# First GLU group split into two blocks, transposes placed inside later products, and nine products on zeros ahead of the first

## The chip, the cores and the metric

The kernel runs on one core of one Trainium2 chip. The metric is the device time of one execution in microseconds, and the median of three runs is taken. TensorE (PE) has a clock gate with two levels, 1.2 and 2.4 GHz; the profile lists the granted share of the full clock.

## What is computed

One hybrid decoder layer on 256 tokens of width 2048, in float32:

```python
h = rmsnorm(x, pre_mix_norm[l])
z = h @ w_in[l]
conv_in, q_lat, kv_lat, k_rope = z[..., :c1], z[..., c1:c2], z[..., c2:c3], z[..., c3:]
a, g = jnp.split(conv_in, 2, axis=-1)
u = a * jax.nn.sigmoid(g)
u = causal_depthwise_conv(u, conv_w[l], conv_b[l])
u = jax.nn.silu(layernorm(u, conv_ln_g[l], conv_ln_b[l]))
q = (rmsnorm(q_lat, q_norm[l]) @ w_uq[l]).reshape(B, S, N_HEADS, QK_HEAD)
...
kv = (rmsnorm(kv_lat, kv_norm[l]) @ w_ukv[l]).reshape(B, S, N_HEADS, QK_NOPE + V_HEAD)
...
attn = causal_attention(q_full, k_full, v)
mix = jnp.concatenate([rmsnorm(u, conv_out_norm[l]),
                       rmsnorm(attn, attn_out_norm[l])], axis=-1) @ w_out[l]
x = x + rmsnorm(mix, post_mix_norm[l])
hf = rmsnorm(x, pre_ffn_norm[l])
ff = (jax.nn.silu(hf @ w_gate[l]) * (hf @ w_up[l])) @ w_down[l]
x = x + rmsnorm(ff, post_ffn_norm[l])
```

The conv has 1024 channels and 31 taps; there are 8 heads with 128 plain and 64 rotary query columns; the q latent has 768 columns, the kv latent 512.

## The kernel before

**Products.** Every operand is split into two float16 parts, high and low, whose sum is the operand. A weight arrives by DMA in pieces of at most 2048 columns by 128 partitions, in one of four stage buffers; ACT writes the high part (line 97) and DVE the low part (line 98) into eight pairs of buffers. `mm3` (lines 136 to 144) makes a token-major product: for each of 16 row tiles and each of two token blocks three matmuls (high by high, high by low, low by high), 96 matmuls for a product of 2048 rows. `mm3t` (lines 146 to 153) does the same feature-major. All weight DMAs are issued by SP, in one queue; a piece's DMA waits for a stage buffer, which is free when DVE has made the low part of four pieces before.

**Order of the early work.** In program order:
1. x transposed is loaded in pieces and split (lines 102 and 103, `load_x`) between the pieces of the first weight group, `wg0` (pieces of 1, 1, 2, 2, 2, 4 and 4 row tiles). Then `wg1` is loaded, and ahead of its third piece both halves of x by tokens (line 206), which the token norm needs (lines 248 to 254).
2. Four GLU groups of 512 columns (256 values and 256 gates, two channel blocks of 128). After a group's product, for each token block: tanh of the gates (line 298), a copy of the values (line 300), u = (tanh + 1) * values on DVE (line 302), two transposes on PE (line 305) into PSUM, and a copy into the padded channel-major buffer `upad` (line 306).
3. The conv works channel-major on `upad`. `conv_todo` is a list of tap tasks; a task is one tap on two channel blocks. Tap 0 runs on ACT (line 270); taps 4, 8, ... 28 are multiplied on ACT (line 281) and added on DVE (line 283, 512 columns at once); the others are one multiply-add on DVE for each block (line 275). `pump(n)` takes the next n tasks off the list, and `PUMPS` gives the counts by place: after the four GLU groups, after the three latent products, after the rotary queries, the values and each head.
4. Three latent products of 448 columns. Their columns are copied by ACT (line 348). The q latent's norm follows the second product, the kv latent's the third: sum of squares on ACT (line 328), rsqrt on GpSimd (line 196), scaling on DVE (line 330), a split, and a DMA transpose of each token block issued by SP (line 332).
5. The shared rotary key: seven small operations on DVE for each token block (lines 364 to 370), a transpose on PE (line 371), a copy (line 372). Then the rotary queries: one product of 36 matmuls, six DVE operations for each token block (lines 387 to 392), four transposes (line 395). Then the values: two products of 24 matmuls on the normed kv latent (lines 402 to 408).
6. Eight heads (projections, scores, softmax scaled by GpSimd on line 467, output), then output projection, layer norm of the conv output, and the feed-forward part. The feed-forward products take the time from about 310 us on.

**What sets the order.** The program text gives each instruction its priority; a planner orders each engine's queue when the program is built, by priority among what it holds to be ready at that time by its own costs. So PE's queue may hold transposes between products that come later in the text, and DVE's may hold later splits ahead of earlier taps. On the chip each queue runs in that fixed order, and an instruction that waits holds everything behind it.

Of the kernel before, what the change touches and what calls it, by code (L numbers as in the profile page):

```python
# [35 lines left out]
PUMPS = dict(conv=(3, 8, 13, 14), lat=(11, 16, 9), v=(1, 0), uqp=3, head=(2, 7, 4, 8, 4, 4, 9, 8))  # L36
# [5 lines left out]
# Exact power-of-two scales that centre the half-precision parts of an operand.  # L42
# [8 lines left out]
def hymba_layer(ctx: ExitStack, tc: tile.TileContext, x, xT, pos, inv_freq, g_pre, w_in, w_lat,  # L51
# [16 lines left out]
    def region(kb, shape, dtype=F32):  # L68
        """A part of the arena from kb KB on; parts with disjoint lifetimes share it."""
# [12 lines left out]
    def nm(base):  # L82
        uid[0] += 1
        return f"{base}_{uid[0]}"
# [15 lines left out]
    def split_g(hi, lo, src, g):  # L100
        """Split of src times a scalar per partition."""
        nc.scalar.activation(hi, src, AF.Copy, scale=g)  # L102
        nc.vector.scalar_tensor_tensor(lo, src, g, hi, op0=ALU.mult, op1=ALU.subtract)

    class Weights:
        """Columns of a weight, on chip as half-precision parts, in blocks of kpb row tiles."""
# [6 lines left out]
        def load(self, src, scale, first=None, before=None):  # L113
            """src: [P, kt * n] with row tile by row tile along the free axis."""
# [31 lines left out]
    def mm3t(ps, x_of, wgt, c0):  # L146
        """Feature-major product of 128 columns: ps += w[:, c0:c0+128].T @ x."""
# [43 lines left out]
    def rstd_of(ss, n, w=1, out_tile=None):  # L191
        """(ss / n + eps) ** -0.5"""
# [24 lines left out]
    ps0 = [acc_tile(), acc_tile()]  # L217
    mm3(ps0, h_of, wg0)
    pos_f = const.tile([P, NTB], F32, name="pos_f")
# [45 lines left out]
    def conv_tap(quarter, k):  # L265
        """One tap of a quarter of the channels, on the vector engine or shared with the scalar engine."""
        cbs = range(2 * quarter, 2 * quarter + 2)
# [15 lines left out]
        nc.vector.tensor_tensor(a, a, t, op=ALU.add)  # L283
# [5 lines left out]
    for j in range(4):  # L289
        if j == 0:  # L290
            ps = ps0
        else:
            wgt = wg1 if j == 1 else Weights(KD, 512).load(w_in[j], W_S)
            ps = [acc_tile(), acc_tile()]
            mm3(ps, h_of, wgt)
        for tb in range(NTB):
            th = work.tile([P, 256], F32, tag="A", name=nm("th"), bufs=3)
            nc.scalar.activation(th, ps[tb][:, 256:512], AF.Tanh, scale=r_half[:, tb : tb + 1])
            av = work.tile([P, 256], F32, tag="B", name=nm("av"), bufs=3)
# [476 lines left out]
```

## Time and profile before

| | us |
|---|---|
| runs: median, lowest, highest | 1021.41, 1021.18, 1021.69 |
| the profiled execution: span from first to last instruction | 1019.8 |
| PE busy (matmuls, pipelined) | 988.7 |
| DVE busy | 635.8 |
| ACT busy | 502.6 |
| GpSimd (POOL) busy | 37.2 |

The profiled execution has no time of its own on record beside its span; the span is 1.6 us under the median of the runs. In the rows, L142 is a line of the kernel, PEld is PE's weight load, which overlaps the matmuls, and a row of several instructions ends in x and their number. The duration of a matmul holds its way through the array, so matmuls that follow each other overlap on record. The idle time of an engine before an instruction, and what ended it, stand in square brackets.

### The profile page before, as it was taken

The numbers are of one execution on the slowest core, as the hardware profiler recorded it, in microseconds if no ns is written. First come the engines' busy times: TensorE is split into PE (matmuls) and PEld (weight loads), VectorE is DVE, ScalarE is ACT, GpSimd is POOL, SyncE is SP. The second block draws the span as 40 slices with busy tenths as digits, with TensorE's granted clock in tenths as the row PEclk, the third lists the DMA queues.
The fourth block names the chain that finished last, engine by engine and source line by source line (L and its number), as shares of the span: only waits on it lengthen the run. The fifth ranks groups of instructions, "written<-read, shape, count | busy, mean of one in ns | idle before, by whom it ended". The sixth has DMA issues, their size and how long they took to land.

```text
span 1019.8 us, 11876 instructions
## 1 busy us (share of the span) xinstructions
PE 988.7 (97%) x4712; PEld 468.2 (46%) x4712; DVE 635.8 (62%) x724; ACT 502.6 (49%) x577; POOL 37.2 (4%) x50
## 2 busy tenths in 40 slices
PE   6999997999999999999999999999999999999996
PEld 2444553774444444444444444444444444444442
DVE  6699999999859874555555555554455444454412
ACT  7796665664747564444444444444444333343400
POOL 0000000034100100000000000000000000000000
PEclk9999998999999999999999999999999999999998
DMA  9874666577546978667666766677766665556302
GB/s 345 326 258 141 220 210 193 165 248 239 174 165 170 294 287 298 210 206 223 216 215 218 220 218 217 218 203 228 214 209 208 213 204 204 202 207 206 124 1 83
DMA packets 69512, 214.21 MB, mean 210 GB/s; under 512 B 41808, under 2 KB 42448, under 8 KB 47440
## 3 DMA queue, kind: packets, MB, share of 16 engines
q1 hardware_dynamic: 68736, 212.52, 63.6%
q8 instruction: 37, 0.61, 0.3%
q10 hardware_dynamic: 720, 0.93, 0.3%
q14 instruction: 19, 0.16, 0.0%
HBM read 202.16 MB, written 2.10 MB: 200 GB/s over the span
## 4 chain that ended last, share of the span: by engine, by line
PE 74%; DVE 11%; issue 4%; ACT 3%; POOL 2%; DMA 1%; DVEq 0%; POOLq 0%; ACTq 0%; SPq 0%
PE acc L144 23%; PE acc L143 23%; PE acc L142 23%; DVE wlo L98 3%; DVE arena L275 3%; ACT whi L97 1%; DVE arena L283 1%; POOL sm L196 1%; PE tmp L151 1%; PE tmp L152 1%; PE tmp L153 1%; POOL ss L467 1%; PE acc L448 1%; PE acc L447 1%; POOL arena L486 0%
## 5 line engine op out<-in xcount | busy, mean ns | idle before, releaser
L98 DVE SCALAR_TENSOR_TENSOR wlo<-st,whi 128x2048 f16<-128x2048 f32 (+4 forms) x191 | 419.7, 2200 | 281.6 <-ACT whi L97 281.6
L142 PE MATMUL acc<-whi,arena 128*128 128x512 f16 (+1 forms) x1436 | 543.9, 379 | 5.5 <-ACT whi L97 5.4
L143 PE MATMUL acc<-wlo,arena 128*128 128x512 f16 (+1 forms) x1436 | 544.0, 379 | 3.5 <-DVE wlo L98 3.4
L144 PE MATMUL acc<-whi,arena 128*128 128x512 f16 (+1 forms) x1436 | 543.5, 379 | 0.0
L97 ACT ACTIVATE whi<-st 128x2048 f16<-128x2048 f32 (+4 forms) x191 | 350.4, 1837 | 321.8 <-PE acc L144 291.0
L142 PEld LDWEIGHTS <-arena 128*128 128x128 f16 x1436 | 141.3, 98 | 172.0 <-ACT arena L102 4.9
L144 PEld LDWEIGHTS <-arena 128*128 128x128 f16 x1436 | 141.1, 98 | 170.7 <-issue 6.5
L143 PEld LDWEIGHTS <-arena 128*128 128x128 f16 x1436 | 140.9, 98 | 167.1 <-issue 3.1
L275 DVE SCALAR_TENSOR_TENSOR arena<-arena 128x256 f32<-128x256 f32 x184 | 78.0, 481 | 0.0
L621 ACT ACTIVATE sg<-acc,r_f 128x256 f32<-128x256 f32 x44 | 20.8, 475 | 58.4 <-PE acc L144 58.4
L623 DVE SCALAR_TENSOR_TENSOR a<-acc,r_f,sg 128x256 f32<-128x256 f32 x44 | 21.2, 483 | 20.6 <-ACT sg L621 20.6
L281 ACT ACTIVATE x_sb<-arena 128x256 f32<-128x256 f32 x56 | 25.4, 507 | 12.0 <-DVE arena L283 12.0
L652 ACT ACTIVATE junk<-acc 128x512 bf16<-128x512 f32 x8 | 4.8, 597 | 46.9 <-PE acc L144 46.8
L663 POOL TENSOR_TENSOR sm<-sm,neg_half 128x1 f32<-128x1 f32 x2 | 1.1, 540 | 663.3 <-DVE sm L661 663.3
L661 DVE TENSOR_SCALAR sm<-ssd,sm 128x1 f32<-128x1 f32 x2 | 0.4, 214 | 34.3 <-ACT junk L652 34.3
L151 PE MATMUL tmp<-arena,whi 128*128 128x256 f16 x80 | 21.8, 273 | 0.0
L153 PE MATMUL tmp<-arena,wlo 128*128 128x256 f16 x80 | 21.8, 273 | 0.0
L152 PE MATMUL tmp<-arena,whi 128*128 128x256 f16 x80 | 21.8, 273 | 0.0
L196 POOL TENSOR_TENSOR sm<-sm,neg_half 128x1 f32<-128x1 f32 (+1 forms) x12 | 11.9, 994 | 250.0 <-DVE sm L194 250.0
L98 DVE SCALAR_TENSOR_TENSOR ahl<-a,ahl 128x256 f16<-128x256 f32 x44 | 18.3, 417 | 2.5 <-ACT ahl L97 2.5
L97 ACT ACTIVATE ahl<-a 128x256 f16<-128x256 f32 x44 | 17.7, 406 | 3.9 <-DMA arena<-hl 3.9
L283 DVE TENSOR_TENSOR arena<-arena,x_sb 128x512 f32<-128x512 f32 x28 | 19.1, 681 | 0.1
(145 smaller groups left out, 329.4 us busy)
## 6 DMA issues: line engine op xcount, KB each, us to landing
st<-in_w_gu SPq DMA_DIRECT2D x88, 1024.0 KB, 5.1
st<-in_w_dn SPq DMA_DIRECT2D x44, 1024.0 KB, 4.8
st<-in_w_out SPq DMA_DIRECT2D x16, 1024.0 KB, 5.4
st<-in_w_in SPq DMA_DIRECT2D x14, 1024.0 KB, 9.3
st<-in_w_lat SPq DMA_DIRECT2D x12, 896.0 KB, 4.6
x_sb<-in_x SPq DMA_DIRECT2D x4, 1024.0 KB, 8.6
st<-in_w_uqn SPq DMA_DIRECT2D x4, 768.0 KB, 4.6
st<-in_w_uv SPq DMA_DIRECT2D x2, 1024.0 KB, 6.7
```

Source lines behind the costliest of these rows:

```text
L97: nc.scalar.activation(hi, src, AF.Copy, scale=scale)
L98: nc.vector.scalar_tensor_tensor(lo, src, scale, hi, op0=ALU.mult, op1=ALU.subtract)
L142: nc.tensor.matmul(p_ap, xh, wh, start=(start and k == 0), stop=False)
L143: nc.tensor.matmul(p_ap, xh, wl, start=False, stop=False)
L144: nc.tensor.matmul(p_ap, xl, wh, start=False, stop=(stop and k == wgt.kt - 1))
L151: nc.tensor.matmul(ps, wh[:, c0 : c0 + P], xh, start=(k == 0), stop=False)
L152: nc.tensor.matmul(ps, wh[:, c0 : c0 + P], xl, start=False, stop=False)
L153: nc.tensor.matmul(ps, wl[:, c0 : c0 + P], xh, start=False, stop=(k == wgt.kt - 1))
L196: nc.gpsimd.tensor_tensor(r, t, neg_half.to_broadcast([P, w]), op=ALU.pow)
L275: nc.vector.scalar_tensor_tensor(cacc[:, cb, :], upad[:, cb, k : k + S], cw[:, cb, k : k + 1], cacc[:, cb, :], op0=ALU.mult, op1=ALU.add)
L281: nc.scalar.activation(t[:, i, :], upad[:, cb, k : k + S], AF.Copy, scale=cw[:, cb, k : k + 1])
L283: nc.vector.tensor_tensor(a, a, t, op=ALU.add)
```

## The change

- The first GLU group's weights are split into two halves, `wg0` and `wg0b`, each with 128 value and 128 gate columns, so one channel block each. The first half's product accumulates in two buffers of the other PSUM pool.
- x by tokens is loaded half ahead of the second and half ahead of the third piece of `wg1`.
- A GLU group is cut in two steps: `glu` makes u after the product; `turn` does the transposes, the copies into `upad` and the pump. `mm3` takes a table `at` of such steps by row tile of a later product: the first half's at row tile 6 and the second half's at row tile 10 of the second group's product, the others' at row tile 3 of the product behind theirs.
- Tap tasks name their channel blocks: one block for the two halves, two for the others. There are now 62 tasks of one block and 93 of two; before, 124 of two. The pump counts are set anew.
- The rotary key's transposes move behind the values' products. The rotary queries are made for the first token block ahead of the values' first product and turned behind it; the second block follows in the same way by the second.
- At the start a buffer is set to zero, ACT copies one of its columns, and PE does nine products of 512 columns on it.
- Comments are taken out.

```diff
-PUMPS = dict(conv=(3, 8, 13, 14), lat=(11, 16, 9), v=(1, 0), uqp=3, head=(2, 7, 4, 8, 4, 4, 9, 8))
+PUMPS = dict(conv=(12, 22, 22, 15, 14), lat=(11, 16, 9), v=(1, 0), uqp=3, head=(1, 5, 3, 5, 3, 3, 5, 5))
...
-    def mm3(ps, x_of, wgt, tbs=(0, 1), k0=0, start=True, stop=True):
+    def mm3(ps, x_of, wgt, tbs=(0, 1), k0=0, start=True, stop=True, at=None):
         for k in range(wgt.kt):
+            if at and k in at:
+                at[k]()
             wh, wl = wgt.parts[k]
...
+    idle = region(20, (512,), F16)
+    nc.vector.memset(idle, 0.0)
+    nc.scalar.activation(idle[:, 0:1], idle[:, 0:1], AF.Copy)
+    warm = tmp_tile()
+    for i in range(9):
+        nc.tensor.matmul(warm, idle[:, 0:P], idle, start=True, stop=True)
     gpre = const.tile([P, KD], F32, name="gpre")
...
-    wg0 = Weights(KD, 512).load(w_in[0], W_S, first=[1, 1, 2, 2, 2, 4, 4], before=load_x)
+    wg0 = Weights(KD, 256).load(w_in0[0], W_S, first=[1, 1, 2, 2, 2, 4, 4], before=load_x)
     h_of = flat(hpool_h, hpool_l)
+    wg0b = Weights(KD, 256).load(w_in0[1], W_S)
     def load_tokens(k0, k1):
-        if k0 == 8:
-            for tb in range(NTB):
-                nc.sync.dma_start(x_sb[:, tb, :], x[:, tb, :])
-    wg1 = Weights(KD, 512).load(w_in[1], W_S, before=load_tokens)
+        if k0 in (4, 8):
+            nc.sync.dma_start(x_sb[:, k0 // 4 - 1, :], x[:, k0 // 4 - 1, :])
+    wg1 = Weights(KD, 512).load(w_in[0], W_S, before=load_tokens)
...
-    ps0 = [acc_tile(), acc_tile()]
+    ps0 = [tmp_tile()[:, :256], tmp_tile()[:, :256]]
     mm3(ps0, h_of, wg0)
+    ps1 = [acc_tile()[:, :256], acc_tile()[:, :256]]
+    mm3(ps1, h_of, wg0b)
...
-    for j in range(4):
-        if j == 0:
-            ps = ps0
-        else:
-            wgt = wg1 if j == 1 else Weights(KD, 512).load(w_in[j], W_S)
-            ps = [acc_tile(), acc_tile()]
-            mm3(ps, h_of, wgt)
...
-        conv_todo += [(j, k) for k in range(TAPS)]
-        pump(PUMPS["conv"][j])
+    def glu(cbs, ps, n_pump):
+        n = len(cbs) * P
+        us = []
+        for tb in range(NTB):
+            th = work.tile([P, 256], F32, tag="A", name=nm("th"), bufs=3)[:, :n]
+            nc.scalar.activation(th, ps[tb][:, n : 2 * n], AF.Tanh, scale=r_half[:, tb : tb + 1])
+            av = work.tile([P, 256], F32, tag="B", name=nm("av"), bufs=3)[:, :n]
+            nc.scalar.activation(av, ps[tb][:, 0:n], AF.Copy, scale=r_half[:, tb : tb + 1])
...
             nc.vector.scalar_tensor_tensor(u, th, 1.0, av, op0=ALU.add, op1=ALU.mult)
+            us.append(u)
+        def turn():
+            for tb, u in enumerate(us):
+                tp = tmp_tile()
+                for i in range(len(cbs)):
+                    nc.tensor.transpose(tp[:, i * P : (i + 1) * P], u[:, i * P : (i + 1) * P], ident)
+                nc.scalar.copy(upad[:, cbs[0] : cbs[-1] + 1, PAD + tb * P : PAD + (tb + 1) * P],
+                               tp[:, :n].rearrange("p (c t) -> p c t", t=P))
+            conv_todo.extend((cbs, k) for k in range(TAPS))
+            pump(n_pump)
+        return turn
+    turns = {6: glu((0,), ps0, PUMPS["conv"][0]), 10: glu((1,), ps1, PUMPS["conv"][1])}
+    for j in range(1, 4):
+        wgt = wg1 if j == 1 else Weights(KD, 512).load(w_in[j - 1], W_S)
+        ps = [acc_tile(), acc_tile()]
+        mm3(ps, h_of, wgt, at=turns)
+        turns = {3: glu((2 * j, 2 * j + 1), ps, PUMPS["conv"][j + 1])}
...
-        mm3(ps, h_of, wgt)
+        mm3(ps, h_of, wgt, at=turns if j == 0 else None)
...
-        nc.tensor.transpose(tp[:, TB[tb]], kp.rearrange("p a b -> p (a b)"), ident)
-    nc.scalar.copy(kpT, tp[:, :S])
+        kps.append(kp)
     wgt = Weights(QL // P, 512).load(w_uqp, W_S)
     ps = [acc_tile(), acc_tile()]
     mm3(ps, lat_of(qn), wgt)
...
+    qp = rotary_query(0)
     pump(PUMPS["uqp"])
     for j in range(2):
         wgt = Weights(KL // P, 512).load(w_uv[j], W_S)
+        ps_v = [acc_tile(), acc_tile()]
+        mm3(ps_v, lat_of(kvn), wgt)
+        for tb in range(NTB):
+            nc.scalar.activation(v_sb[:, tb, j * 512 : (j + 1) * 512], ps_v[tb], AF.Copy, scale=U)
+        if j == 0:
+            turn_queries(0, qp)
+            qp = rotary_query(1)
         pump(PUMPS["v"][j])
+    tp = tmp_tile()
+    for tb in range(NTB):
+        nc.tensor.transpose(tp[:, TB[tb]], kps[tb].rearrange("p a b -> p (a b)"), ident)
+    nc.scalar.copy(kpT, tp[:, :S])
+    turn_queries(1, qp)
...
-    a["w_in"] = np.stack([_tiles(w, c) for c in groups])
+    a["w_in"] = np.stack([_tiles(w, c) for c in groups[1:]])
+    a["w_in0"] = np.stack([_tiles(w, np.r_[P * j : P * j + P, C + P * j : C + P * j + P]) for j in range(2)])
```

`rotary_query` holds what stood on lines 380 to 392, `turn_queries` what stood on lines 393 to 397.

## Rows read from the trace of the kernel before

**Rows 1.** By stretch: PE, PEld, DVE, ACT, POOL busy (instructions); clock; DMA; GB/s.
```profile
0.00:38.80 38.80, 30.80 (x129) 13.19 (x130) 21.26 (x30) 26.86 (x37) 2.35 (x13) 1.00 0.95 367
...
38.80:163.30 124.50, 115.94 (x576) 56.39 (x575) 120.93 (x203) 91.34 (x130) 2.81 (x4) 0.99 0.63 213
...
163.30:190.00 26.70, 26.70 (x148) 15.48 (x147) 26.60 (x55) 16.72 (x27) 0.00 (x0) 0.92 0.57 168
...
181.00:250.00 69.00, 65.27 (x415) 46.06 (x414) 64.22 (x140) 41.73 (x88) 23.22 (x25) 0.98 0.63 209
```

**Rows 2.** Timeline of the start.
```profile
3.07 1.28 ACT L102 ACT_TABLE_LOAD   x1 [3.07 <-DMA arena<-in_xT]
...
5.45 0.58 PE L142 MATMUL acc<-whi,arena 128*128 128x512 f16 x1 [5.45 <-ACT whi L97]
...
8.26 0.63 PE L142 MATMUL acc<-whi,arena 128*128 128x512 f16 x1
...
8.68 0.63 PE L143 MATMUL acc<-wlo,arena 128*128 128x512 f16 x1
...
21.79 0.38 PE L143 MATMUL acc<-wlo,arena 128*128 128x512 f16 x1 [1.46 <-DVE wlo L98]
```

**Rows 3.** Timeline of the rotary stage, PE, ACT and DVE.
```profile
155.09 1.06 ACT L97 ACTIVATE whi<-st 128x1024 f16<-128x1024 f32 x1 [3.94 <-DMA st<-in_w_uk]
...
158.75 0.61 ACT L348 ACTIVATE arena<-acc,r_x 128x448 f32<-128x448 f32 x1
...
161.73 0.75 DVE L330 SCALAR_TENSOR_TENSOR arena<-arena,sm 128x512 f32<-128x512 f32 x1 [0.34 <-POOL sm L196]
...
162.70 0.47 PE L371 MATMUL tmp<-ident,kp 128*128 128x128 f32 x1 [5.56 <-DVE kp L370]
...
163.39 0.63 PE L142 MATMUL acc<-whi,arena 128*128 128x512 f16 x1
...
167.74 0.38 PE L143 MATMUL acc<-wlo,arena 128*128 128x512 f16 x1
...
170.11 0.38 PE L142 MATMUL acc<-whi,arena 128*128 128x512 f16 x1
```

**Rows 4.** Waits of PE: us in total, times, longest.
```profile
PE tmp L305 <- DVE u L302: 3.0, 3, 1.2
...
PE tmp L473 <- POOL ss L467: 2.3, 2, 2.0
```

**Rows 5.** DVE by line to 161.7 us: busy us, mean ns, idle before.
```profile
L103 DVE SCALAR_TENSOR_TENSOR arena<-arena,gpre 128x256 f16<-128x256 f32 x16 | 6.9, 480 | 3.5 <-ACT arena L102 3.5
```

**Rows 6.** Timeline of DVE: rotary tables, a weight split, taps.
```profile
45.52 0.94 DVE L237 SCALAR_TENSOR_TENSOR arena<-arena 128x128 f32<-128x128 f32 x3
...
76.34 2.28 DVE L98 SCALAR_TENSOR_TENSOR wlo<-st,whi 128x2048 f16<-128x2048 f32 x1
...
81.99 0.68 DVE L283 TENSOR_TENSOR arena<-arena,x_sb 128x512 f32<-128x512 f32 x1
...
82.59 3.24 DVE L275 SCALAR_TENSOR_TENSOR arena<-arena 128x256 f32<-128x256 f32 x8
```

**Rows 7.** Timeline of GLU, first group on PE, last on ACT and DVE.
```profile
42.08 0.38 PE L305 MATMUL tmp<-ident,u 128*128 128x128 f32 x2
...
97.40 0.47 ACT L298 ACTIVATE th<-acc,r_half 128x256 f32<-128x256 f32 x1 [3.67 <-PE acc L144]
...
100.11 0.74 DVE L302 SCALAR_TENSOR_TENSOR u<-th,av 128x256 f32<-128x256 f32 x2
```

**Rows 8.** DMA issues to 200 us: median us from issue to landing.
```profile
arena<-arena SPq DMA_TRANSPOSE x4, 3.6
```

**Rows 9.** Single lines, taps to 189.9 us and tables: ns least, median, most; starts.
```profile
L275 DVE SCALAR_TENSOR_TENSOR arena<-arena x139: 466/471/480, 49.1 to 189.5; 128x256 f32<-128x256 f32 x139
...
L283 DVE TENSOR_TENSOR arena<-arena,x_sb x21: 672/677/692, 51.6 to 188.9; 128x512 f32<-128x512 f32 x21
...
L237 DVE SCALAR_TENSOR_TENSOR arena<-arena x3: 291/292/293, 45.5 to 46.2; 128x128 f32<-128x128 f32 x3
```

More of the change, by code (lines that the diff above doesn't have):

```diff
@@ L50, in hymba_layer @@
 @with_exitstack
-def hymba_layer(ctx: ExitStack, tc: tile.TileContext, x, xT, pos, inv_freq, g_pre, w_in, w_lat,
+def hymba_layer(ctx: ExitStack, tc: tile.TileContext, x, xT, pos, inv_freq, g_pre, w_in0, w_in, w_lat,
                 q_norm, w_uqn, w_uqp, kv_norm, w_uk, w_uv, conv_w, conv_v, g_attn,
@@ L263, in hymba_layer, with conv_tap @@
     prod_n = [0]
-    def conv_tap(quarter, k):
-        cbs = range(2 * quarter, 2 * quarter + 2)
+    def conv_tap(cbs, k):
         if k == 0:
@@ L282, in conv_tap @@
         a = cacc[:, cbs[0] : cbs[-1] + 1, :]
-        nc.vector.tensor_tensor(a, a, t, op=ALU.add)
+        nc.vector.tensor_tensor(a, a, t[:, : len(cbs)], op=ALU.add)
     def pump(n):
@@ L287, in pump @@
             conv_tap(*conv_todo.pop(0))
-    for j in range(4):
-        if j == 0:
-            ps = ps0
-        else:
-            wgt = wg1 if j == 1 else Weights(KD, 512).load(w_in[j], W_S)
-            ps = [acc_tile(), acc_tile()]
-            mm3(ps, h_of, wgt)
-        for tb in range(NTB):
-            th = work.tile([P, 256], F32, tag="A", name=nm("th"), bufs=3)
-            nc.scalar.activation(th, ps[tb][:, 256:512], AF.Tanh, scale=r_half[:, tb : tb + 1])
-            av = work.tile([P, 256], F32, tag="B", name=nm("av"), bufs=3)
-            nc.scalar.activation(av, ps[tb][:, 0:256], AF.Copy, scale=r_half[:, tb : tb + 1])
-            u = work.tile([P, 256], F32, tag="C", name=nm("u"), bufs=2)
-            nc.vector.scalar_tensor_tensor(u, th, 1.0, av, op0=ALU.add, op1=ALU.mult)
-            tp = tmp_tile()
-            for i in range(2):
-                nc.tensor.transpose(tp[:, i * P : (i + 1) * P], u[:, i * P : (i + 1) * P], ident)
-            nc.scalar.copy(upad[:, 2 * j : 2 * j + 2, PAD + tb * P : PAD + (tb + 1) * P],
-                           tp[:, : 2 * P].rearrange("p (c t) -> p c t", c=2))
-        conv_todo += [(j, k) for k in range(TAPS)]
-        pump(PUMPS["conv"][j])
@@ new lines, in glu @@
+    def glu(cbs, ps, n_pump):
+        n = len(cbs) * P
+        us = []
+        for tb in range(NTB):
+            th = work.tile([P, 256], F32, tag="A", name=nm("th"), bufs=3)[:, :n]
+            nc.scalar.activation(th, ps[tb][:, n : 2 * n], AF.Tanh, scale=r_half[:, tb : tb + 1])
+            av = work.tile([P, 256], F32, tag="B", name=nm("av"), bufs=3)[:, :n]
+            nc.scalar.activation(av, ps[tb][:, 0:n], AF.Copy, scale=r_half[:, tb : tb + 1])
+            if cbs == (1,):
+                u = work.tile([P, P], F32, tag="kp", name=nm("u"))
+            else:
+                u = work.tile([P, 256], F32, tag="C", name=nm("u"), bufs=2)[:, :n]
+            nc.vector.scalar_tensor_tensor(u, th, 1.0, av, op0=ALU.add, op1=ALU.mult)
+            us.append(u)
[9 more added lines that the diff above has]
+        return turn
@@ L354, in hymba_layer @@
     latent_norm(z_kv, g_kv, KL, kv_hl, kvn)
+    qpT = region(8, (H // 2, S))
     kpT = region(33, (S,))
-    tp = tmp_tile()
+    kps = []
     for tb in range(NTB):
@@ L378, in hymba_layer, with rotary_query @@
     mm3(ps, lat_of(qn), wgt)
-    for tb in range(NTB):
+    def rotary_query(tb):
         zq = work.tile([P, H, ROPE], F32, tag="ss", name=nm("zq"), bufs=3)
@@ L392, in hymba_layer, with turn_queries @@
         nc.vector.tensor_tensor(qp[:, :, HALF:ROPE], qp[:, :, HALF:ROPE], t1[:, :, HALF:ROPE], op=ALU.add)
+        return qp
+    def turn_queries(tb, qp):
         tp = tmp_tile()
```

6 lines of the change are left out of this document (1 added, 5 removed).

## The prediction

> **What bounds the kernel now.** I read the times, then the busy time by stretch, then what PE waits for, then the order of instructions around the places that the change touches. Two engines share the first 250 us. TensorE (PE) is nearly dense, and so is VectorE (DVE): from 38.8 to 163.3 us PE is busy 115.94 and DVE 120.93 of 124.5 us, from 163.3 to 190 both all but the whole time [rows 1]. Before 38.8 us DVE worked 21.26 us only, while the DMA engines were 0.95 busy [rows 1]. From about 290 us on PE is fed almost without breaks, so what is won or lost earlier reaches the end one to one. In the early part PE loses time in four places:
> - The start. The first product comes at 5.45 us, behind a table load of 1.28 us on ScalarE (ACT) and the first splits; its products of 512 columns follow each other every 0.42 us and are on record with 0.63 us each [rows 2]. Later they last 0.38 us and follow every 0.215 us (eleven from 167.74 to 170.11) [rows 3]. These are the two levels of the clock, 1.2 and 2.4 GHz; some eleven products are slow. A wait of 1.46 us for a weight's low part follows at 21.79 [rows 2].
> - GLU transposes: three waits for the product u, 3.0 us in all [rows 4].
> - The rotary key's transposes: 5.56 us of waiting before 162.70, then eleven products at the slow level again (0.63 us on record, so 11 x 0.21 = 2.3 us lost) [rows 3]. Together 7.9 us.
> - The heads: from 181 to 250 us PE is idle 69.0 - 65.3 = 3.7 us [rows 1], 2.0 of it in one wait for GpSimd's scaling of the scores [rows 4].
>
> **Start: -1.5 us.** Removed: ACT's table load from the path, since an early Copy triggers it, and half the bytes and half of PE's work ahead of the first finished product. Added: a memset and nine products on zeros. They stand in front of the real ones on PE: 9 x 0.42 = 3.8 us from about 1 us on, so the first real product can't come before about 4.8 us; 0.6 us is won there. Where the clock then rises earlier, up to eleven products' 0.21 us are won, 2.3 us; no row shows what products on zeros do to the clock. But the splits become the limit: per row tile DVE makes a low part of x (0.48 us [rows 5]) and one of 256 weight columns (an eighth of the 2.28 us of a full split [rows 6], 0.29), 0.77 us against six products of 256 columns, 0.65 us if their time goes by columns. So PE waits some 16 x 0.12 = 1.9 us in the first half, and up to a split's 2.28 us at the start of the second, where it waited 1.46 before. Cutting 96 products into 192 is taken at nothing by the same rule; PE's slack in the splits covers it. The DMA bytes are the same, in the same 38.8 us that are full already [rows 1]; on SP's queue x's first half now goes out one megabyte of weights earlier, its second behind one more piece. Bounds: 0 (DMA alone sets the pace) to -4.4 (the 0.6, the clock's 2.3 and the 1.46). I stay in the lower half because DMA and splits are the nearer limit.
>
> **GLU: -2.1 us.** The transposes go from the product's end to three row tiles into the next one: 18 products, 18 x 0.215 = 3.9 us later. For the last group the first tanh starts at 97.40, when its product is done, and both u stand at 100.11 + 0.74 = 100.85, 3.5 us later [rows 7]. So its wait goes. For the group ahead of which ACT reloads its table (1.28 us, as at the start) 3.5 + 1.3 - 3.9 = 0.9 us stays. Bounds: 0 (the third rival) to -3.0. The added small operations of a fifth group fall on ACT, which is idle 33 of 124.5 us [rows 1].
>
> **Rotary: -1.5 us.** The key's transposes move behind the values' products, so the 5.56 us wait is gone from where it stands, and the 22 products between 162.70 and 170.11 can run at once, done by about 157 + 22 x 0.215 = 162 us. But next in line are the values' products, which need the kv latent after its norm and its DMA transposes. That norm's step on DVE came at 161.73 and the values' first product ran at 170.11 [rows 3]: 8.4 us, of which the DMA transposes take 3.6 [rows 8]. So the wait moves to 162 to 170, and only what the norm comes earlier is won. The norm hangs on ACT's copy of the latent columns at 158.75, behind a weight split that had waited 3.94 us for its DMA at 155.09 [rows 3]. Bounds: -4.4 (the copy right behind its product, about 154.3) to +5.4 (last rival). Slow products can come again after such a wait; I leave them in. The rotary queries are turned in two halves, each with 24 products (5.2 us) of the values beside their work on DVE.
>
> **DVE's load: +1.5 us.** The pump counts bring conv taps forward. Ahead of the kv norm they were 38 + 36 pairs of blocks, 148 block taps; now they are 62 single ones and 59 pairs, 180. The price of 32 more: a cycle of four pair taps is six operations of 0.395 us (eight in 3.24 us, less the last one's 0.47) and one of 0.60 [rows 6], 2.97 us for eight block taps, so 11.9 us more before the heads and as much less in them. The cover: by 189.9 us DVE had done 139/2 + 21 = 90.5 pair taps [rows 9] where 75 were due (78 pumped, three of them first taps on ACT), a lead of 15.5 x 0.74 = 11.5 us. The 11.9 use that cover up. On top, the 62 single taps work on one block each, so every one depends on the one just before. Three such dependent operations take 0.94 us [rows 6] and last 0.292 each [rows 9]: (0.94 - 0.29)/2 = 0.325 from start to start, 0.03 more than one lasts, while independent taps start 0.08 before the last one ends [rows 6]. A dependent tap so costs 0.11 us more; 46 of the 62 are of this kind on DVE, 5.1 us if nothing stands between them. Against that, the first taps come some 8 us earlier, into the 17.5 us that DVE was idle before 38.8 [rows 1]; I take 3.5 as regained. 5.1 - 3.5 = 1.6, taken as 1.5. Bounds: -3.5 to +5.1.
> The Trainium skill's page "VectorE: DVE Perf Modes", section "The DRAIN you can't avoid", says that the next operation can't issue until the pipe is empty, and that chaining doesn't change it. By it dependent taps would cost nothing extra, and this term would be -3.5. The trace does not bear that wording out: independent taps start before the last one ends [rows 6].
>
> **Heads: -1 us.** DVE has 11.9 us less there, but arrives without its lead. PE's longest wait was for GpSimd beside a busy DVE; fewer taps in the last heads (5 for 9 and 5 for 8) may shorten it. Bounds: 0 to -3.7.
>
> **Sum.** -1.5 - 2.1 - 1.5 + 1.5 - 1.0 = -4.6 us. The profiled span is 1019.8 us and the runs' median 1021.41, so 1.6 us lie outside the span and stay. I predict 1021.4 - 4.6 = 1016.8 us.
>
> **Rivals.**
> - *Nearly everything is won*: dependent taps cost nothing, the copy of the latents comes right behind its product, the heads' waits go. -3 - 3 - 4.4 - 2 = -12.4, some 1009 us. For it: PE's losses add up to more than that. Against: DVE has only 3.6 us idle in 124.5 [rows 1]. Chance 0.16.
> - *DVE sets the end*: PE's gains turn into waits for splits further on, since DVE is as full as PE. DVE's own sum is +5.1 - 3.5, less 1 to 3 of idle in the heads, about 0: 1021 us, 1019.4 to 1023.4. For it: [rows 1]. Against: the lead of 11.5 us. Chance 0.20.
> - *The order does not change much*: a planner sets each engine's order when the program is built, and it had put the first group's transposes into the next product by itself (42.08, without a wait) [rows 7]. If it leaves the later groups as they were, 2.1 us stay lost: 1019 us. Chance 0.08.
> - *Slower*: the kv norm stands behind the taps on DVE's queue. Place: the step that came at 161.73 [rows 3]. DVE brings 11.9 + 5.1 - 3.5 = 13.5 us more to that point. Splits of later weights that it had done ahead of it (five, up to 2.28 us each, 9.8 together at most) can move behind it; 3.7 to 5.4 us cannot. The values' products follow it by 8.4 us, so they come that much later whatever PE won before, and the heads give back 1: 1021.4 + 5.4 - 1 = 1026 us. It decides once that step comes later than about 165 us. Chance 0.14.
>
> **How the numbers follow.** The forecast as worked out, 1012 to 1019, has 0.42. About 0.2%, 2 us, is what a measurement of this kernel can tell from no change. Faster: 0.42 + 0.16 + 0.08 = 0.66; same 0.20; slower 0.14. The range from 1008.5 to 1023.5 takes in the forecast, the second and third rival and the larger part of the first; it leaves out the slower one and the first one's tail.
>
> **What would show it.** In the changed kernel: products on zeros from about 1 us, the first real product near 4.8 us and the 0.215 us pace before 8; no wait of PE on u over 0.9 us; the wait that stood before 162.70 now in front of the values' products, with the kv norm's step on DVE between 155 and 163; DVE without breaks from 36 us on, single-block taps 0.5 us apart. I am wrong if PE runs through the rotary stage without a wait (then it is faster than I say), or if PE waits for low parts in the latent products or the kv norm comes after 165 (then it is slower).

## The result, and the profile after

The changed kernel takes 1033.98 us (median of four runs, 1033.16 to 1035.77); the kernel before took 1021.29 us beside it (four runs). The ratio is 1.0128, 95% interval 1.0113 to 1.0142: 12.7 us slower. The forecast was 1016.8 us, its range ended at 1023.5, and faster had 0.66. The profiled execution took 1035.77 us (span 1034.0), the longest of the four, so it shows about 1.8 us more than the median. Times of whole kernels below are medians, places inside a kernel are those of its profiled execution; a loss is the median less that of the kernel before measured beside it (1021.3 to 1021.9 us).

By stretch, with the columns of [rows 1]:

```profile
0.00:38.80 38.80, 31.95 (x227) 22.80 (x228) 23.30 (x34) 28.47 (x45) 2.34 (x13) 1.00 0.94 367
38.80:163.30 124.50, 120.07 (x598) 58.50 (x596) 121.55 (x207) 88.63 (x128) 1.64 (x2) 1.00 0.61 199
163.30:190.00 26.70, 17.44 (x90) 9.12 (x88) 24.75 (x63) 13.67 (x24) 1.58 (x2) 0.81 0.44 134
```

DVE did 2.0 us more work before 38.8 us, but that is three more low parts of weights (12 in place of 9); no tap was among them. The third line has a hole: PE is busy 17.4 of 26.7 us where it was busy throughout, and the clock is 0.81 in place of 0.92. Not all of that is a loss, since the wait of 5.56 us before 162.70 [rows 3] ended just ahead of this stretch. How late the changed kernel is, place by place, is seen from four instructions: the first product of the second GLU group, the first product of the rotary queries, the first copy of the values, and the first gate of the feed-forward part. Before:

```profile
31.72 0.38 PE L142 MATMUL acc<-whi,arena 128*128 128x512 f16 x1
153.96 0.38 PE L142 MATMUL acc<-whi,arena 128*128 128x512 f16 x1
175.36 1.16 ACT L407 ACTIVATE arena<-acc 128x512 f32<-128x512 f32 x2
341.25 0.45 ACT L621 ACTIVATE sg<-acc,r_f 128x256 f32<-128x256 f32 x1
```

and in the changed kernel:

```profile
33.25 0.38 PE L145 MATMUL acc<-whi,arena 128*128 128x512 f16 x1
156.90 0.38 PE L145 MATMUL acc<-whi,arena 128*128 128x512 f16 x1
180.75 1.25 ACT L432 ACTIVATE arena<-acc 128x512 f32<-128x512 f32 x2 [4.55 <-PE acc L147]
354.15 0.45 ACT L654 ACTIVATE sg<-acc,r_f 128x256 f32<-128x256 f32 x1
```

It is 1.5, 2.9, 5.4 and 12.9 us late, and 14.2 us at the end of the span. So more than half is lost behind the values. What PE waits for, over the whole span (beside [rows 4]):

```profile
PE acc L145 <- DMA arena<-arena: 9.3, 1, 9.3
PE acc L146 <- DVE wlo L98: 6.2, 3, 2.5
PE tmp L505 <- POOL ss L500: 3.1, 1, 3.1
...
PE tmp L319 <- DVE u L312: 1.7, 2, 1.5
```

The wait for the rotary key (5.56 us, [rows 3]) is gone and one of 9.3 us for the kv latent's DMA transposes stands in front of the values. The waits for u fell from 3.0 to 1.7 us only. Of the three waits of line 146 for low parts, 1.14 us at 22.99 stands where 1.46 stood, 2.55 us at 80.40 is new, and 2.51 us at 358.88 in the first feed-forward products was 1.03. The timeline shows the places; first the start and the GLU stage, PE, ACT and DVE (answering [rows 2] and [rows 7]):

```profile
2.70 4.02 PE L170 MATMUL tmp<-arena 128*128 128x512 f16 x9 [2.70 <-ACT arena L167]
6.52 0.42 PE L145 MATMUL tmp<-whi,arena 128*128 128x256 f16 x1
...
22.99 0.27 PE L146 MATMUL acc<-wlo,arena 128*128 128x256 f16 x1 [1.14 <-DVE wlo L98]
...
56.76 1.28 ACT L305 ACT_TABLE_LOAD   x1
58.05 0.47 ACT L305 ACTIVATE th<-acc,r_half 128x256 f32<-128x256 f32 x1
...
57.70 2.28 DVE L98 SCALAR_TENSOR_TENSOR wlo<-st,whi 128x2048 f16<-128x2048 f32 x1
59.91 0.48 DVE L285 SCALAR_TENSOR_TENSOR arena<-arena 128x256 f32<-128x256 f32 x1
60.30 0.41 DVE L312 SCALAR_TENSOR_TENSOR u<-th,av 128x256 f32<-128x256 f32 x1
...
60.77 0.44 PE L319 MATMUL tmp<-ident,u 128*128 128x128 f32 x2 [1.45 <-DVE u L312]
...
78.06 2.28 DVE L98 SCALAR_TENSOR_TENSOR wlo<-st,whi 128x2048 f16<-128x2048 f32 x1
...
80.40 0.38 PE L146 MATMUL acc<-wlo,arena 128*128 128x512 f16 x1 [2.55 <-DVE wlo L98]
80.61 0.38 PE L147 MATMUL acc<-whi,arena 128*128 128x512 f16 x1
```

Ahead of 33.25 stand 9 products on zeros and 192 halves; the divided group loses 1.5 us. The second group's tanh stands behind a weight split and a table load on ACT, and its u behind a split and a tap on DVE, so the transposes wait although they were put later (the split on ACT starts at 54.85). From 61.31 to 78.06 DVE did nothing but taps, and the low part that PE needed at 77.9 came at 80.4. Then the rotary stage, DVE, ACT and PE (answering [rows 3]):

```profile
163.58 2.46 DVE L285 SCALAR_TENSOR_TENSOR arena<-arena 128x256 f32<-128x256 f32 x6
165.96 0.14 DVE L203 TENSOR_SCALAR sm<-sm 128x1 f32<-128x1 f32 x1
...
167.24 0.75 DVE L353 SCALAR_TENSOR_TENSOR arena<-arena,sm 128x512 f32<-128x512 f32 x1 [0.43 <-POOL sm L205]
167.90 2.46 DVE L285 SCALAR_TENSOR_TENSOR arena<-arena 128x256 f32<-128x256 f32 x6
170.28 0.68 DVE L98 SCALAR_TENSOR_TENSOR arena<-arena 128x512 f16<-128x512 f32 x1
...
171.77 0.75 DVE L353 SCALAR_TENSOR_TENSOR arena<-arena,sm 128x512 f32<-128x512 f32 x1 [0.44 <-POOL sm L205]
...
164.00 0.19 ACT L351 ACTIVATION_READ_ACCUMULATOR junk<-arena 128x1 f32 x1
...
165.93 1.49 ACT L97 ACTIVATE whi<-st 128x1536 f16<-128x1536 f32 x1 [1.34 <-DMA st<-in_w_uqn]
167.31 0.61 ACT L351 ACTIVATE junk<-arena 128x512 bf16<-128x512 f32 x1
...
174.10 0.61 PE L145 MATMUL acc<-whi,arena 128*128 128x512 f16 x1 [9.26 <-DMA arena<-arena]
```

The kv norm's step (161.73 before) comes at 167.24, its second at 171.77. The second came at 163.29 before:

```profile
163.29 0.75 DVE L330 SCALAR_TENSOR_TENSOR arena<-arena,sm 128x512 f32<-128x512 f32 x1 [0.44 <-POOL sm L196]
```

The first sum of squares stood at 164.2, but its short DVE step waits behind six taps until 165.96; the low part behind six more; the second sum of squares waits on ACT behind a weight split whose DMA is late. The values begin at 174.10 in place of 170.11.

Behind the values the largest single loss stands at 226 us. Two short waits, 0.49 us at 225.49 and 0.62 us, are followed by the slow level of the clock (1.2 GHz, granted 0.50); the kernel before has 1.00 at the same work. The changed kernel's lines, then that of the kernel before, in the columns of [rows 1]:

```profile
226.57 1.22 PE L511 MATMUL tmp<-pT,arena 128*128 128x256 f32 x2 [0.62 <-ACT pT L509]
...
226.00:232.00 6.00, 5.43 (x23) 3.99 (x24) 4.49 (x12) 2.10 (x7) 1.79 (x3) 0.50 0.84 306
```

```profile
216.00:222.00 6.00, 5.87 (x41) 4.62 (x42) 5.55 (x16) 2.92 (x9) 1.88 (x4) 1.00 0.74 244
```

Counted by the projections' products there, one by one, the changed kernel falls from 7.0 us behind (219.12, before 212.09) to 11.1 (232.88, before 221.76).

### The profile page after: what moved, and what is told of

It is laid out like the page before. It is cut to its first block, busy times and chain, and to the rows that moved or that the text cites. A ratio compares the mean times of both kernels' runs of the same rounds, so it can differ in the third digit from the quotient of the medians.

```text
span 1034.0 us, 12115 instructions
## 1 busy us (share of the span) xinstructions
PE 996.0 (96%) x4817; PEld 480.8 (46%) x4817; DVE 637.5 (62%) x736; ACT 504.6 (49%) x586; POOL 33.0 (3%) x50
## 4 chain that ended last, share of the span: by engine, by line
PE 73%; DVE 13%; issue 7%; ACT 2%; DMA 2%; POOL 1%; SPq 0%; DVEq 0%; POOLq 0%; ACTq 0%
PE acc L146 24%; PE acc L147 24%; PE acc L145 23%; DVE wlo L98 4%; DVE arena L285 4%; DVE arena L293 1%; DMA st<-in_w_in 1%; POOL ss L500 1%; POOL sm L205 1%; ACT whi L97 1%; ACT arena L102 0%; DMA arena<-in_xT 0%; DMA arena<-hl 0%; PE tmp L511 0%; DVE x_sb L631 0%
## 5 line engine op out<-in xcount | busy, mean ns | idle before, releaser
L145 PE MATMUL acc<-whi,arena 128*128 128x512 f16 (+2 forms) x1436 | 539.6, 376 | 9.3 <-DMA arena<-arena 9.3
L146 PE MATMUL acc<-wlo,arena 128*128 128x512 f16 (+2 forms) x1436 | 539.9, 376 | 6.2 <-DVE wlo L98 6.2
L147 PE MATMUL acc<-whi,arena 128*128 128x512 f16 (+2 forms) x1436 | 540.1, 376 | 0.0
L145 PEld LDWEIGHTS <-arena 128*128 128x128 f16 x1468 | 144.4, 98 | 175.3 <-DMA arena<-arena 9.8
L147 PEld LDWEIGHTS <-arena 128*128 128x128 f16 x1468 | 144.1, 98 | 173.1 <-issue 10.7
L146 PEld LDWEIGHTS <-arena 128*128 128x128 f16 x1468 | 144.1, 98 | 163.5 <-issue 2.2
L291 ACT ACTIVATE x_sb<-arena 128x256 f32<-128x256 f32 x56 | 25.2, 498 | 14.2 <-DVE arena L293 14.1
L154 PE MATMUL tmp<-arena,whi 128*128 128x256 f16 x80 | 22.9, 286 | 0.0
L155 PE MATMUL tmp<-arena,whi 128*128 128x256 f16 x80 | 22.8, 285 | 0.0
L97 ACT ACTIVATE ahl<-a 128x256 f16<-128x256 f32 x44 | 17.7, 406 | 5.6 <-DMA arena<-hl 5.6
L293 DVE TENSOR_TENSOR arena<-arena,x_sb 128x512 f32<-128x512 f32 (+1 forms) x35 | 20.3, 581 | 0.1
```

The source lines that it names most:

```text
L97: nc.scalar.activation(hi, src, AF.Copy, scale=scale)
L145: nc.tensor.matmul(p_ap, xh, wh, start=(start and k == 0), stop=False)
L146: nc.tensor.matmul(p_ap, xh, wl, start=False, stop=False)
L147: nc.tensor.matmul(p_ap, xl, wh, start=False, stop=(stop and k == wgt.kt - 1))
L154: nc.tensor.matmul(ps, wh[:, c0 : c0 + P], xh, start=(k == 0), stop=False)
L155: nc.tensor.matmul(ps, wh[:, c0 : c0 + P], xl, start=False, stop=False)
```

## Experiments

**Which part loses.** Each of these runs undoes one part of the change, or makes one part alone.

The taps of the changed kernel put back:

```diff
-PUMPS = dict(conv=(12, 22, 22, 15, 14), lat=(11, 16, 9), v=(1, 0), uqp=3, head=(1, 5, 3, 5, 3, 3, 5, 5))
+PUMPS = dict(conv=(3, 3, 16, 26, 21), lat=(11, 16, 9), v=(1, 0), uqp=3, head=(2, 7, 4, 8, 4, 4, 9, 8))
```

> The changed kernel with as many block taps before each stage as the kernel before had (conv 3, 3, 16, 26, 21: 76 block taps ahead of the latents in place of 108; heads 2, 7, 4, 8, 4, 4, 9, 8). Theory (the 32 block taps brought forward make VectorE late for the kv norm, and the values wait for it): the norm's two steps come at 160 to 164 us in place of 167 and 172, the wait of 9.6 us before the values' first product falls to 5 or less, the waits for low parts near 80 us go, and the time is 1016 to 1022 us. Rival (the moved rotary work or the split group is at fault): the time stays above 1030 us.

Measured 1029.04, loss 7.7 us (ratio 1.0074, 1.0051 to 1.0097). The norm's steps came at 163.5 and 166.4, the waits before the values were 3.8 and 1.7 us. So, each kernel in the order that the planner gives it, the forward taps cost 5 us of the 12.7, and something else is wrong too: neither number came.

The rotary section of the kernel before put into the changed kernel (the diff's part from `qpT` to `turn_queries(1, qp)` undone; one line of it):

```diff
-    turn_queries(1, qp)
+        nc.tensor.transpose(tp[:, TB[tb]], kp.rearrange("p a b -> p (a b)"), ident)
```

> The changed kernel with the rotary stage in the order of before (key transposes and rotary queries ahead of the values). Theory (taps brought forward): the kv norm still comes after 165 us and the time stays at 1030 to 1037 us. Rival (the rotary move is at fault: it lays the values' products open to the kv norm and loses the clock): the time falls to 1018 to 1024 us.

Measured 1033.05, loss 11.7 (1.0097 to 1.0127): the rotary move is not at fault.

The same part of the diff alone, made in the kernel before:

> The kernel before with the rotary move alone. Theory (taps brought forward are at fault): a gain of 0 to 3 us, 1018 to 1022 us, the kv norm at 160 to 164 us. Rival (the rotary move is at fault): 1027 us or more.

Measured 1021.82, loss 0.4 (1.000 to 1.0019). The wait moved as foreseen, 6.2 us in front of the values' products, and wins nothing.

The taps alone brought forward, in the kernel before:

```diff
-PUMPS = dict(conv=(3, 8, 13, 14), lat=(11, 16, 9), v=(1, 0), uqp=3, head=(2, 7, 4, 8, 4, 4, 9, 8))
+PUMPS = dict(conv=(17, 11, 12, 14), lat=(11, 16, 9), v=(1, 0), uqp=3, head=(1, 5, 3, 5, 3, 3, 5, 5))
```

> The kernel before with only as many block taps brought forward as in the changed kernel (conv 17, 11, 12, 14 pairs, 108 block taps ahead of the latents; heads 1, 5, 3, 5, 3, 3, 5, 5); taps stay in pairs. Theory (taps brought forward are at fault): the kv norm after 165 us and a loss of 7 to 13 us, 1028 to 1034 us. Second theory (only the dependent one-block taps make VectorE late): 1021 to 1024 us. Rival (rotary move or split): 1020 to 1022 us.

Measured 1039.04, loss 17.7 (1.0119 to 1.019): more than the whole change. Its taps are in pairs, so the loss needs no dependent taps.

The zeros alone in the kernel before (`+`), and the changed kernel without them (`-`):

```diff
+    idle = region(20, (512,), F16)
...
+        nc.tensor.matmul(warm, idle[:, 0:P], idle, start=True, stop=True)
```

> The kernel before with only the memset, the early Copy on ScalarE and the nine products on zeros. Theory (the start is set by the DMAs): 1020 to 1022 us, the gain of the earlier full clock lost again in waits for weights and x before 25 us. Rival (the clock alone cost 2 to 3 us there): 1018 to 1019 us.

> The changed kernel without the memset, the early Copy and the nine products on zeros. Theory (the start is set by the DMAs, so the zeros win nothing): 1033 to 1036 us. Rival (the zeros win the slow products at the start): 1036 to 1038 us; second rival (the zeros stand in the way of the first real products): 1031 to 1033 us.

Measured 1021.61, loss -0.2 (0.9993 to 1.0012), and 1031.49, loss 9.7 (1.0084 to 1.0114). Alone the zeros do nothing. The changed kernel is 2.5 us longer with them than without, but not because they stand in the way of the first real products: 0.45 us of that shows at the end of the first group, and at 228 us the profiled execution with zeros is 0.4 us ahead. They part behind it: the clock from 226 to 232 us is 0.50 with the zeros and 0.72 without, and the wait for a low part in the first feed-forward products is 2.51 us with them (358.88) and 1.47 without (356.84). No run shows why.

Late transposes alone, for undivided groups in the kernel before:

```diff
-            mm3(ps, h_of, wgt)
+        mm3(ps, h_of, wgt, at=turns)
+        turns = {3: glu(j, ps)}
```

> The kernel before with only the four GLU groups' transposes given out late (six row tiles into the second group, three into the later products), group 0 undivided, pump counts as before. Theory: the waits for u (3 us in all) go from TensorE, 1018 to 1021 us. Rival (VectorE's or ScalarE's queue sets the pace there, so that nothing is won): 1021 to 1023 us.

Measured 1026.2, loss 4.4 (1.0025 to 1.0068): both numbers missed. PE's waits for u fell to 0.3 us, and the first values copy came 2.1 us earlier than before; then the profiled execution lost 4 us behind 195 us. The same came when three parts that lose nothing ahead of the heads were put together (zeros, late transposes, rotary move; group undivided, taps as before):

> The kernel before with three parts of the change (products on zeros, late GLU transposes, moved rotary work), the first group undivided and the taps where they were. Theory (the division of the first group and the forward taps make all of the loss): 1019 to 1023 us, group 1's first product near 31 us. Rival (late transposes or the rotary move start the loss, through the order that the planner gives the heads): 1026 us or more.

Measured 1028.83, loss 7.0 (1.0046 to 1.0086). By the first values copy it was 1.3 us ahead. Its diff is the three above together.

Four more shifted the taps or one step of the change. In the changed kernel, with old counts and the first two blocks joined after three taps each:

```diff
-            conv_todo.extend((cbs, k) for k in range(TAPS))
+                conv_todo.extend((cbs, k) for k in range(3))
+                conv_todo.extend(((0, 1), k) for k in range(3, TAPS))
```

> The changed kernel with the block taps before each stage as in the kernel before, and the first two blocks joined again after three single taps each (conv 3, 3, 8, 13, 14; heads as before). Theory (what is left of the loss with the old pump counts is the dependent one-block taps, 46 or so on VectorE at 0.1 us each): kv norm steps 3 to 5 us earlier than with single taps, time 1019 to 1024 us. Rival (the loss left comes from the start, the split of the group or the moved rotary work): 1027 to 1031 us as with single taps.

Measured 1039.46, loss 17.7 (1.0147 to 1.0203). Its kv norm came only 2 to 3 us later than before and its first values copy 1.7 us, but 18 us more went up to the first feed-forward gate (361.30 in place of 341.25); as a test of dependent taps it says nothing.

```diff
-PUMPS = dict(conv=(12, 22, 22, 15, 14), lat=(11, 16, 9), v=(1, 0), uqp=3, head=(1, 5, 3, 5, 3, 3, 5, 5))
+PUMPS = dict(conv=(12, 22, 22, 15, 14), lat=(11, 9, 0), v=(1, 0), uqp=3, head=(2, 7, 4, 8, 4, 4, 9, 8))
```

> The changed kernel with its forward taps in the GLU stage, but 16 pairs fewer between the latent products (lat 11, 9, 0) and as many more in the heads (2, 7, 4, 8, 4, 4, 9, 8): the block taps ahead of the kv norm are again 148. Theory (VectorE's sum of work ahead of the kv norm decides): the norm's steps at 160 to 165 us, the wait before the values under 6 us, the wait for a low part near 80 us stays (2 to 3 us), time 1026 to 1030 us as with the old counts. Rival (the taps in the GLU stage decide): 1032 us or more.

Measured 1033.12, loss 11.3 (1.0093 to 1.0135): the rival's number. With the sum of taps ahead of the kv norm as before, its step still came at 165.93, and the loss is that of the changed kernel within the spread of the runs. So the taps brought into the GLU stage are enough for it; there the low part at 81 us (a wait of 2.55 us) and u (1.79 us) come late.

```diff
-    csum = region(16, (S,))
+    csum = region(51, (S,))
```

> The changed kernel with the layer norm's first sum kept behind the last head on VectorE (its result lies where the last heads' values were, so it can't be written before they have been used). Theory (the sum of 3.7 us ahead of the last head's softmax makes TensorE's stop of 3.2 us at 254 us and the slow products behind it): that stop goes, 1029 to 1032 us. Rival (the stop is only moved: the layer norm comes later and TensorE waits for it): 1033 to 1036 us.

Measured 1033.24, loss 11.4 (1.009 to 1.0128), between the two numbers. PE's wait of 3.07 us before 254.64 became 1.61 us before 244.75 and 0.90 us before 258.54, so that sum is a small part.

In the kernel before:

```diff
-PUMPS = dict(conv=(3, 8, 13, 14), lat=(11, 16, 9), v=(1, 0), uqp=3, head=(2, 7, 4, 8, 4, 4, 9, 8))
+PUMPS = dict(conv=(10, 10, 12, 14), lat=(11, 16, 9), v=(1, 0), uqp=3, head=(1, 6, 3, 7, 4, 3, 7, 7))
```

> The kernel before with half as many taps brought forward, 16 block taps (conv 10, 10, 12, 14; heads 1, 6, 3, 7, 4, 3, 7, 7), still in pairs. Threshold theory (a lead of 15 pairs covers the first half, as the prediction held): 1020 to 1024 us. Linear theory (each tap ahead of a due step delays it, no cover): half of the 17 us, 1028 to 1032 us.

Measured 1032.46, loss 10.6 (1.0081 to 1.0115): no threshold. But TensorE was only 1.6 us late at the first values copy and 11.5 at the feed-forward products: most of it went behind the taps' place, so this run does not size the cover.

**The order behind.** Late transposes alone and the three parts together were ahead at the first values copy and lost 4 to 10 us behind it. The planner had given them another order from the first head on, though their text there is the same. So I held that order with edges of issue order (no semaphore), from the heads to the first feed-forward product:

```diff
+        for first, then in zip(line, line[1:]):
+            tc.add_manual_dep(then, first.name, info, reason="order")
```

where `line` is one engine's instructions (PE, DVE, ACT, POOL) in the order of the other kernel.

> The kernel before, nothing changed but the order of the four engines' instructions from the first head to the feed-forward products, which is the one that the planner gave to the kernel with zeros, late transposes and moved rotary work. Theory (the order alone makes the loss): 1027 to 1031 us. Rival (the order is harmless): 1020 to 1023 us.

Measured 1027.77, loss 6.3 (1.0037 to 1.0071). The kernel before, in another order of the same instructions, is 6 us slower.

> The kernel with zeros, late GLU transposes and moved rotary work in one (group undivided, taps where they were), and from the first head to the feed-forward products each engine's instructions held in the order that they have in the kernel before. Theory (the planner's other order in the heads and the output projection makes the loss of 7 us): 1019 to 1022 us, the mean of the stage as before. Rival (the loss comes from what arrives late or from the slow clock, whatever the order): 1027 to 1030 us.

Measured 1020.40, loss -1.1 (0.9983 to 1.0002), against 7.0 in the planner's own order.

> The kernel before with the late GLU transposes alone, and the order of the kernel before held from the first head on. Theory (the 1 to 2 us that late transposes win in the GLU stage are kept when the order behind is): 1018.5 to 1020.5 us, faster than both kernels. Rival: 1022 us or more, as with the planner's own order.

Measured 1020.36, loss -1.1 (0.9977 to 0.9995): late transposes with the old order held are faster than the kernel before by 0.05 to 0.23%, and faster than the changed kernel.

What the order does, as PE's waits from 190 to 300 us of the kernel before in the new order:

```profile
PE tmp L514 <- POOL arena L498: 2.4, 1, 2.4
PE tmp L555 <- DVE arena L550: 2.1, 1, 2.1
PE acc L459 <- ACT kT L445: 2.0, 2, 1.8
```

and in its own order:

```profile
PE tmp L473 <- POOL ss L467: 2.3, 2, 2.0
PE acc L447 <- ACT kT L433: 1.1, 2, 1.0
```

All rows of the view add up to 8.8 us in the new order and 4.9 in its own. Small products of the norms (lines 514 and 555) hold PE's queue until POOL or DVE has done their operand. The profiled execution in the new order was the longest of its four, and its span is 8.5 us over that of the kernel before; beside the 3.9 us of waits the clock makes up most of the rest. The kernel before in the new order, columns as above:

```profile
250.00:300.00 50.00, 46.37 (x198) 20.82 (x197) 36.66 (x29) 30.30 (x35) 2.10 (x3) 0.91 0.54 194
```

and in its own:

```profile
250.00:300.00 50.00, 48.44 (x230) 22.45 (x228) 39.12 (x33) 31.20 (x38) 3.60 (x3) 1.00 0.59 208
```

From 250 to 300 us 32 products fewer are done at a clock of 0.91 in place of 1.00; 0.09 of 50 us is 4.5 us, as an estimate.

**The change at one order.** The last runs complete four combinations, all with zeros, late transposes, the moved rotary work and the order of before held:

> The changed kernel with each engine's instructions from the first head to the feed-forward products held in the order of the kernel before (less the 16 pairs of taps that are done earlier). Theory (of the 12.7 us some 6 are lost before the heads and the rest by the other order behind them): 1026 to 1029 us. Rival (the late arrival makes the later losses too): 1032 us or more.

> The whole change, first group divided, but as many block taps ahead of each stage as before, and the old order held from the first head on. Beside the runs at that same order without the division (1020.4 us) and with both division and forward taps (1033.0 us) it gives the price of the division alone. Theory (the division loses the 1.6 us at the start and 1.5 to 2 us more up to the heads): 1023 to 1026 us. Rival (the division is the greater part): 1028 us or more.

> Zeros, late transposes, moved rotary work and the 32 block taps brought forward (in pairs), the first group undivided, the old order held from the first head on. It gives the price of the forward taps alone at that order. Theory (VectorE has no cover for them): 1028 to 1032 us. Rival (the old order and the undivided group leave cover enough): 1020 to 1024 us.

| loss, us | taps where they were | 32 block taps forward |
|---|---|---|
| group undivided | -1.1 | +11.0 (1.0096 to 1.0126) |
| group divided | +3.9 (1.0026 to 1.0054) | +11.5 (1.010 to 1.013) |

The changed kernel in the planner's own order loses 12.7. So my theory for it (half from the order) fell: there the order is worth 1.2 us. The forward taps cost 12.1 us by themselves and 7.6 where the group is divided; the division costs 5.0, or 0.5 beside the taps, perhaps because both delay the same values. One reserve is large. Up to the values the taps cost 3 to 5 us: the first values copy comes at 180.66 in place of 177.34 in the divided runs, and at 177.07 in place of 174.10 in the undivided ones, where the last copy is 5.1 us late. The rest is lost behind, though DVE has fewer taps there. In the undivided run it is one place: PE waits 3.7 us for a projection before 196.18, slow products follow, and by 203.68 the lag is 12.0 us. The divided run waits 1.7 us there, the changed kernel in its own order 0.8 at most for a projection. So these 7 us may belong to an old order that doesn't fit taps that are done already, and not to DVE's work ahead of the values.

## Why the prediction was wrong

By the places above, the terms came out so, in the profiled executions: start +1.5 us (forecast -1.5), GLU +1.4 (-2.1), rotary and DVE's load together +2.5 up to the first values copy (0), and behind it +8.8 (heads, -1). Three of them lie outside the bounds that I gave them.

**DVE's load** is the step that failed first. The load was right (32 block taps, 11.9 us), the cover was not. With the term at +1.5 us the lead was to cover all of it; at one held order the taps cost 7.6 to 12.1 us, 3 to 5 of them up to the values. I counted the lead of taps at 189.9 us: 15.5 pairs, 11.5 us. But the kv norm's step comes at 161.7. The taps of DVE in the kernel before, line 275 and then line 283, to 160 us and from 175 to 190 (busy, count):

```profile
0.00:160.00 160.00, 45.69 (x111) 1.00 0.71 250
...
175.00:190.00 15.00, 9.44 (x23) 1.00 0.52 173
...
0.00:160.00 160.00, 11.51 (x17) 1.00 0.71 250
...
175.00:190.00 15.00, 2.73 (x4) 1.00 0.52 173
```

To 160 us these are 111 + 2 x 17 = 145 block taps, where 142 were due (148 less six first taps, which ACT does). The lead was 3 block taps, some 1.1 us (3 x 0.37). Of the 36 block taps that followed up to 189.9 us, 31 came from 175 on, behind the norm. In the changed kernel DVE had done 158 block taps by 160 us, 13 more, and 4.5 us less of line 98's splits (68.14 against 72.68 us). Those splits are not free to move: PE, ACT's next split and a stage buffer wait for them, as at 80.40 and 165.93.

The 3.5 us that earlier taps were to regain did not come either. The first half's last product starts at 21.37, but its tanh waits for the token norm (`r_half`), as it did before; the first tap on DVE starts when it did before (49.01, below). Before, then the changed kernel:

```profile
36.50 0.47 ACT L298 ACTIVATE th<-acc,r_half 128x256 f32<-128x256 f32 x1 [1.55 <-DVE r_half L254]
...
49.08 2.46 DVE L275 SCALAR_TENSOR_TENSOR arena<-arena 128x256 f32<-128x256 f32 x6
```

```profile
35.47 0.37 ACT L305 ACTIVATE th<-tmp,r_half 128x128 f32<-128x128 f32 x1 [1.55 <-DVE r_half L265]
```

So dividing the product brought u forward by 1 us and the taps by nothing; behind u the first tap on ACT (48.38) stands behind a weight split and a table load.

**The slower rival** had the mechanism and the mark: the step after 165 us. The two steps came 5.5 and 8.5 us late, the values' first product 4.0 and their first copy 5.4, within its 3.7 to 5.4 us. What it had wrong is the part behind: it let the heads give back 1 us, and 8.8 us more were lost there.

**Dependent taps: +5.1 - 3.5.** No such price arose. Judged by their spacing, the planner laid the two chains alternately, so that most neighbours are independent (the trace does not name the block of a tap):

```profile
49.01 1.00 DVE L285 SCALAR_TENSOR_TENSOR arena<-arena 128x256 f32<-128x256 f32 x2
...
76.14 1.67 DVE L285 SCALAR_TENSOR_TENSOR arena<-arena 128x256 f32<-128x256 f32 x4
```

Alternating, four single taps take 1.67 us, 0.40 from start to start; two on one block 1.00 us, 0.52 apart. So a dependent tap does cost 0.12 us more, as worked out, but few were. The Trainium skill's page "VectorE: DVE Perf Modes", section "The DRAIN you can't avoid", says that the next operation does not start until the pipe is empty, and that one which is not held starts earlier. The trace has taps of both kinds: two on one block start 0.52 us apart and last 0.48, the alternating ones start 0.40 apart.

**Start: -1.5; measured +1.5** (33.25 against 31.72). I took DMA and splits as the limit, and did not see what the division does behind them. All of x must now be there for the first half, whose last product starts at 21.37; then 96 half products at 0.109 us, 10.5 us, and a wait of 1.1 follow, which no longer overlap with the arrival of x. The zeros began at 2.70 us, not 1: they wait for the Copy and its table load. So the first real product came at 6.52 us, 1.1 later than before and not 0.6 earlier. The full pace did come sooner, at 7.4 us in place of 10.9, but alone the zeros won nothing (loss -0.2), since the weights and x set the end of the group.

**GLU: -2.1; +1.4.** The mechanism holds for undivided groups (0.3 us of waiting left, and the order held keeps 1.1 us). In the changed kernel the transposes of the second group wait 1.45 us, since tanh and u stand behind splits and a tap, and 2.55 us for a low part is new: 4.3 us of waits in place of 3.0.

**Rotary: -1.5; 0.** The wait moved to where I put it; the kv norm came no earlier, so nothing was won. That was the step's own condition.

**Heads: -1; +8.8 behind the first values copy.** This is the other step that failed, and the larger one in the sum. "What is won or lost earlier reaches the end one to one" did not hold: the same instructions in another order cost 6.3 us there, and in the changed kernel 4.1 us went between 219 and 233 us, most of it to the slow clock behind waits of 0.49 and 0.62 us. I had no term for the clock behind the values. The rival on the planner saw its part only for the GLU transposes.

What stays open: how much of the loss behind the values the forward taps cause, since no run lets DVE do the low parts and the norm's steps ahead of the forward taps; why the first feed-forward products wait 2.3 to 2.8 us for a low part in the divided runs with zeros (358.88 above), 1.47 in the divided run without them, and 1.03 in the undivided ones and before; and what the zeros have to do with that.

## What to carry to other kernels

A lead on a busy engine is cover only if it stands at the moment of the step that it is to protect: count the work done and the work due there, not at the end of the stage. Where a planner orders the queues, an edit reorders stages that it does not touch; compare the planned orders first, and hold the old order behind the edit before judging it. Dividing a stage's first product asks for all of the other operand in half the time, and what follows comes earlier only if the product was its last condition; here the token norm was.

## What the runs showed of the chip

A wait of PE can cost half again as much, or more, in the clock behind it, but not each time. The same wait for the same low part, in the changed kernel (at 80.40 above: 0.21 us to the next product, granted clock 1.00 from 78 to 84 us) and without the zeros (clock 0.72 in that stretch):

```profile
79.94 0.58 PE L146 MATMUL acc<-wlo,arena 128*128 128x512 f16 x1 [2.54 <-DVE wlo L98]
80.33 0.63 PE L147 MATMUL acc<-whi,arena 128*128 128x512 f16 x1
...
83.27 0.38 PE L146 MATMUL acc<-wlo,arena 128*128 128x512 f16 x1
```

Here the eight products from 79.94 on take 3.33 us in place of 8 x 0.215, 1.6 us more (the slow level, 0.43 us apart). In the kernel before in the new order, waits of 1.8 to 2.4 us at 204, 249 and 290 us are each followed by such a stretch, and in the changed kernel waits of 0.49 and 0.62 us at 226 are. So a sum over waits alone can be too small, and a short wait is no sign that the clock stays. Seven of the kernels above spread by 4.1 to 7.5 us from run to run (four or five runs each), the kernel before by 2.9 us in thirteen; whether such waits make the spread is not shown, since the changed kernel and others with them spread by 1.5 to 2.7 us.
